# Gate projections of a decoder trunk as pairs of 64-row matmuls with two banks to add

## The chip, the cores and the metric

The kernel runs on one core of a Trainium2 chip. The metric is the device time of one execution in microseconds. The kernel before has a median of 1394.32 us over three runs (1393.59 to 1394.59).

## What is computed

Two decoder layers over 256 tokens of 1024 features, in float32. Each layer is a half-step feed-forward block, a mixing block and another half-step feed-forward block. The mixing block projects the normalised input with one matrix `w_in`, runs four causal mixers (`nsa`, `ret`, `rwkv`, `swa`) on column groups of the result, projects each mixer's output and sums the four under sigmoid gates. The gates are the last 4 x 1024 columns of the same projection:

```python
p = h @ w_in[l]
gates = sigmoid(c('branch_gate').reshape(B, S, N_BRANCH, D))
merged = (gates[:, :, 0] * (y_nsa @ w_br_nsa[l]) + gates[:, :, 1] * (y_ret @ w_br_ret[l])
          + gates[:, :, 2] * (y_rwkv @ w_br_rwkv[l]) + gates[:, :, 3] * (y_swa @ w_br_swa[l]))
x = x + rms_norm(merged @ w_out[l], mix_post_g[l])
```

## The kernel before

The tokens form two tiles of 128 (`t` = 0, 1). Normalised inputs are held transposed, features on partitions, as two tensors `xhi` and `xlo` of type F32R (lines 209 to 243): a float32 value is the sum of a high and a low part. Weights are streamed from memory in pieces of 128 x 1024 values (`stream`, line 131): a DMA on SyncE's queue into `raw`, then on ScalarE (ACT) a copy into the high part `whi` (line 146), then on VectorE (DVE) the difference `wlo` (line 147). A product of two such pairs is three matmuls that add into one PSUM bank, `mm3` (line 167): high x high (L173), high x low (L174) and low x high (L175).

`bulk_proj` (line 429) is the token-major projection. For each of the 8 chunks of 128 features and each token tile it calls `mm3` with the input as the stationary and 512 weight columns as the moving operand. The result of a token tile is one bank `pj`. When all chunks are in, `evac` takes it out of PSUM. `gate_block` (line 1306) is such a projection: its `evac` is one ACT operation, tanh of half the value, into the tile `gate` (L1309). Sigmoid(x) is 0.5 + 0.5 tanh(x / 2); `branch_block` (line 1313) multiplies its products `z` by gate + 1 on DVE (L1327, L1329) and `acc_split` brings in the factor 0.5 later. A gate block covers 512 columns of one mixer's gate, so there are 8 in each layer, 16 in all.

PSUM has eight banks, in two pools (lines 187 to 191): pool A with three, for projections and branch products, and pool B with five, for transposes, the strands' small products and the output rows (`dn`). A tile waits for a free bank of its pool.

The order of the mixing block is made in two steps. `weave` (line 453) emits work by an estimated clock, `clk`: strands of small, latency-bound products (attention, retention, the RWKV recurrence) as soon as their inputs should be there, and steps of bulk work in between. A projection gives back control after each chunk; `fin` notes when its result is expected. Gate blocks wait for nothing; a branch block waits for its mixer's output and its gate. The framework's scheduler then orders each engine's queue by priority, estimated times and free banks. Each engine runs its queue in that order.

The strands' products use operands of type F32 and often a part of the array: `rs`, `sc`, `lw` and `la` use 64 rows and 128 columns, `pz`, `pu`, `psn`, `py` and `pr` 64 rows and 64 columns. A matmul of F32 operands that is not a transpose shows as two records in the trace, one of F32R operands as one. The profile prints both types of stored operand as f32.

Of the kernel before, what the change touches and what calls it, by code (L numbers as in the profile page):

```python
# [12 lines left out]
AF = mybir.ActivationFunctionType  # L13
# [4 lines left out]
P = 128  # L18
# [9 lines left out]
RD = 1 / 32  # D ** -0.5  # L28
# [7 lines left out]
# per-feature vectors, features on partitions  # L36
V_MU, V_W0, V_A0, V_KK, V_KA, V_RK, V_POS = 0, 8, 10, 12, 14, 16, 18
NV = 18 + 32
# per-feature vectors, broadcast over partitions
# [73 lines left out]
class Trunk:  # L113
# [17 lines left out]
    def stream(self, src, k, n, part=None, between=None):  # L131
        """k chunks of 128 rows by n columns; returns w(chunk, columns) -> (hi, lo)"""
# [20 lines left out]
    def stream2(self, src, part):  # L153
        """one chunk of 1024 columns, its halves' parts in storage of 2 KiB each"""
# [12 lines left out]
    def mm3(self, out, a, b, first, last):  # L167
        """out (+)= a.T @ b with a, b given as (hi, lo) parts."""
        mm = self.nc.tensor.matmul
        d = 3 * max(109.0, 2.5 + b[0].shape[-1] / 2.4)  # L170
        self.clk += d
        self.light = max(0.0, self.light - d)
        mm(out, a[0], b[0], start=first, stop=False)  # L173
        mm(out, a[0], b[1], start=False, stop=False)  # L174
        mm(out, a[1], b[0], start=False, stop=last)  # L175

    def s2(self, shape, name, dt=F32):
        """a slot of up to 2 KiB per partition"""
# [4 lines left out]
    def k1(self, shape, name, dt=F32):  # L183
        """a slot of up to 1 KiB per partition"""
# [15 lines left out]
    def rstd(self, ss, k=1.0):  # L200
        """(sum(ss) + k * eps) ** -0.5 per token, of sums of k / D * x ** 2"""
# [14 lines left out]
    def pre_norm(self, t, xT, ss=None):  # L216
        """x[t] (token-major) -> normalised, transposed, as hi/lo [P, KC, token tile t]; returns the
        part from the transposes on, a step for each half."""
# [31 lines left out]
    def post_norm(self, t, banks, g, half, last):  # L250
        """x[t] += (0.5 if half else 1) * rms_norm(f) * g, f in two PSUM banks; sums of squares of the new x."""
# [28 lines left out]
    def ffn(self, l, wg, wu, wd, xT, post_g, nxt, mix=False, first=None):  # L280
        nc, tc = self.nc, self.tc
        with tc.tile_pool(name=self.nm("ffn"), bufs=1, reuse_waits="tile") as pool:
# [34 lines left out]
            # the first blocks are token-major, so that one token tile's products need not wait for the  # L317
            # other's input
# [53 lines left out]
    def rows_out(self, lhs, wd, g, half, nxt, units, tail, warm=None):  # L372
        """x += norm(lhs.T @ wd), rows of wd streamed in units of (chunks, storage of the parts); the last
        units one token tile after the other, so that the first tile's norms run under the second
        tile's products."""
# [39 lines left out]
    def warm(self, func):  # L415
        """have the table of the next phase's activations loaded while the engine has time"""
# [12 lines left out]
    def bulk_proj(self, l, xT, c0, n, evac, key, lat=900, skew=False):  # L429
        """token-major projection, activations stationary; one step per k-chunk."""  # L430
# [22 lines left out]
    def weave(self, strands, bulk):  # L453
        """Emit work in the order of an estimated clock: latency-bound strands as soon as their
        inputs should be there, bulk products in between."""
# [3 lines left out]
        while live or bulk or cur:  # L459
            ran = False  # L460
            # small products alone let the array's clock drop: bulk at least every so often
# [48 lines left out]
    def rope(self, out_ap, src, t, nh, dup=False):  # L510
        """src [P, nh, HD] (token-major) -> out_ap [P, nh, (2,) HD]."""
# [17 lines left out]
    def transposes(self, srcs):  # L529
        """up to four [P, P] blocks -> one PSUM bank [P, 4, P]."""  # L530
# [10 lines left out]
    def mm4(self, out, a, b):  # L541
        """few columns of b: the array's column groups side by side, as loading a holds them up"""
# [9 lines left out]
    def attention(self, t, groups, score, pv, sink, mask_off, gate, evac):  # L552
        """Groups of two softmaxes: score(g, scores in PSUM, W); pv(j, hh, pT): the pairs (V, p^T) whose
        products make up half hh of chunk j of o^T; evac(t, o^T in PSUM)."""
# [49 lines left out]
    def split_yt(self, yT, u, t, src, from_psum=True):  # L604
        """hi/lo parts of feature-major y (two chunks, one token tile)."""
# [9 lines left out]
    def swa(self, l, xT):  # L615
# [10 lines left out]
        def after(t):  # L626
            r = self.s2([P, 4, HD], "swar")
            # query heads land as 0, 2, 1, 3 so that a pair's halves meet kv heads 0 and 1
# [33 lines left out]
    def nsa(self, l, xT):  # L662
        """two projection blocks (bulk); spawns the strands that follow"""
# [5 lines left out]
        # queries: hi parts above lo parts; keys: hi and lo parts, each twice  # L669
# [81 lines left out]
        def cmp_prep():  # L751
            # 15 overlapping blocks plus position; the last chunk's columns run on into zeros
# [13 lines left out]
        def compress():  # L766
            yield "cmp_x"
            # column group 32 g holds chunks of parity g % 2 of the keys (g < 2) or the values
# [195 lines left out]
    def rwkv_proj(self, l, xT, b):  # L964
        """feature-major projection of 256 columns with token shift"""
# [22 lines left out]
    def rwkv(self, l):  # L988
# [8 lines left out]
        # decay, in-context rate and output gate from the low-rank inputs  # L997
# [20 lines left out]
        # cumulative log decay in each chunk, centred on the chunk's middle  # L1018
# [18 lines left out]
        # normalised removal keys, replacement keys  # L1037
# [44 lines left out]
        # strictly causal / causal interactions within each chunk: rows and columns of one chunk  # L1082
        # share a 64-partition half; units u = (token tile, head pair)
# [21 lines left out]
        # the inverted blocks, at most 32 wide, lie side by side: rows of group g, columns of its block  # L1105
# [27 lines left out]
        # token-major copies  # L1133
# [361 lines left out]
```

## Time and profile before

| what | value |
|---|---|
| median of three runs | 1394.32 us (1393.59 to 1394.59) |
| profiled execution, first to last instruction | 1397.0 us |
| its mean granted TensorE clock | 0.988 |
| PE busy (matmuls) | 1358.2 us, 97% |
| DVE busy | 846.6 us, 61% |
| ACT busy | 644.1 us, 46% |
| chain that ended last, PE's share | 79% |
| moved by DMA | 243.16 MB, mean 174 GB/s |

The profiled execution is known by its span alone; no other time of it is given. A busy share is an average over stages. The busy time of PE is made of modelled ends of overlapping matmuls, so the distance between the starts of two matmuls says more about PE than the duration of one. The mixing blocks run from about 200 to 490 us and from about 900 to 1180 us of the span; the gate tiles are written between 361.4 and 478.9 us and between 1052.8 and 1168.8 us.

### The profile page before, as it was taken

The numbers are of one execution on the slowest core, as the hardware profiler recorded it, in microseconds if no ns is written. First come the engines' busy times: TensorE is split into PE (matmuls) and PEld (weight loads), VectorE is DVE, ScalarE is ACT, GpSimd is POOL, SyncE is SP. The second block draws the span as 40 slices with busy tenths as digits, with TensorE's granted clock in tenths as the row PEclk, the third lists the DMA queues.
The fourth block names the chain that finished last, engine by engine and source line by source line (L and its number), as shares of the span: only waits on it lengthen the run. The fifth ranks groups of instructions, "written<-read, shape, count | busy, mean of one in ns | idle before, by whom it ended". The sixth has DMA issues, their size and how long they took to land.

```text
span 1397.0 us, 26502 instructions
## 1 busy us (share of the span) xinstructions
PE 1358.2 (97%) x10940; PEld 1205.1 (86%) x10940; DVE 846.6 (61%) x1269; ACT 644.1 (46%) x962; POOL 204.9 (15%) x269
## 2 busy tenths in 40 slices
PE   8999999899999999999999999999999999999998
PEld 8999879776778889998899998788777888899986
DVE  6555467758766666554565554677487656655543
ACT  5444456425344455444454444554353445544432
POOL 1000013513332110000000000235035320100000
PEclk9999999899999999999999999999999999999999
DMA  8866553436346546655657556443453565465552
GB/s 273 277 183 187 188 182 99 147 123 197 105 151 194 182 151 209 214 182 181 204 159 240 182 180 198 155 131 124 153 172 99 166 195 189 146 217 185 185 181 76
DMA packets 166153, 243.16 MB, mean 174 GB/s; under 512 B 9216, under 2 KB 120320, under 8 KB 165904
## 3 DMA queue, kind: packets, MB, share of 16 engines
q1 hardware_dynamic: 165248, 239.31, 53.9%
q8 instruction: 86, 1.41, 0.4%
q0 software_dynamic: 352, 1.10, 0.3%
q10 hardware_dynamic: 432, 1.05, 0.2%
q14 instruction: 35, 0.29, 0.1%
HBM read 240.38 MB, written 1.05 MB: 173 GB/s over the span
## 4 chain that ended last, share of the span: by engine, by line
PE 79%; DVE 9%; POOL 4%; ACT 3%; DMA 2%; issue 2%; POOLq 0%; DVEq 0%; SPq 0%; ACTq 0%
PE pg L175 7%; PE pg L173 7%; PE pg L174 7%; PE dn L173 6%; PE dn L175 6%; PE dn L174 6%; PE pj L173 5%; PE pu L174 5%; PE pu L173 5%; PE pu L175 5%; PE pj L175 5%; PE pj L174 5%; DVE wlo L147 2%; PE z L173 1%; PE tr L533 1%
## 5 line engine op out<-in xcount | busy, mean ns | idle before, releaser
L147 DVE TENSOR_TENSOR wlo<-raw,whi 128x1024 fp32r<-128x1024 f32 (+1 forms) x420 | 517.2, 1239 | 385.5 <-ACT whi L146 384.0
L146 ACT ACTIVATE whi<-raw 128x1024 fp32r<-128x1024 f32 (+1 forms) x420 | 436.3, 1046 | 543.7 <-issue 146.3
L173 PE MATMUL pj<-whi,xhi 128*128 128x512 f32 (+2 forms) x448 | 179.5, 401 | 0.4 <-DVE retg L894 0.4
L175 PE MATMUL pj<-whi,xlo 128*128 128x512 f32 (+2 forms) x448 | 173.1, 386 | 0.0
L174 PE MATMUL pj<-wlo,xhi 128*128 128x512 f32 (+2 forms) x448 | 172.6, 385 | 0.0
L173 PE MATMUL pu<-xhi,whi 128*128 128x256 f32 x592 | 168.1, 284 | 0.0
L173 PE MATMUL pg<-xhi,whi 128*128 128x256 f32 x592 | 168.1, 284 | 0.0
L174 PE MATMUL pu<-xlo,whi 128*128 128x256 f32 x592 | 167.8, 283 | 0.0
L175 PE MATMUL pg<-xhi,wlo 128*128 128x256 f32 x592 | 167.8, 283 | 0.0
L175 PE MATMUL pu<-xhi,wlo 128*128 128x256 f32 x592 | 167.8, 283 | 0.0
L174 PE MATMUL pg<-xlo,whi 128*128 128x256 f32 x592 | 167.8, 283 | 0.0
L174 PE MATMUL dn<-wlo,hhi 128*128 128x512 f32 x352 | 137.4, 390 | 0.0
L173 PE MATMUL dn<-whi,hhi 128*128 128x512 f32 x352 | 137.4, 390 | 0.0
L175 PE MATMUL dn<-whi,hlo 128*128 128x512 f32 x352 | 137.1, 390 | 0.0
L204 POOL TENSOR_SCALAR rstd<-ss 128x1 f32<-128x1 f32 x24 | 10.2, 427 | 807.5 <-ACT ja L258 780.3
L174 PEld LDWEIGHTS pg<-xlo,whi 128*128 128x128 f32 x592 | 113.8, 192 | 0.0
L174 PEld LDWEIGHTS pu<-xlo,whi 128*128 128x128 f32 x592 | 113.8, 192 | 0.0
L175 PEld LDWEIGHTS pg<-xhi,wlo 128*128 128x128 f32 x592 | 113.8, 192 | 0.0
L173 PEld LDWEIGHTS pg<-xhi,whi 128*128 128x128 f32 x592 | 113.8, 192 | 0.0
L173 PEld LDWEIGHTS pu<-xhi,whi 128*128 128x128 f32 x592 | 113.8, 192 | 0.0
L175 PEld LDWEIGHTS pu<-xhi,wlo 128*128 128x128 f32 x592 | 113.8, 192 | 0.0
L173 PEld LDWEIGHTS pj<-whi,xhi 128*128 128x128 f32 x448 | 86.2, 192 | 23.5 <-issue 6.6
(349 smaller groups left out, 2268.5 us busy)
## 6 DMA issues: line engine op xcount, KB each, us to landing
raw<-in_w_in_dram SPq DMA_DIRECT2D x112, 512.0 KB, 3.5
raw<-in_ffn_w_gate_dram SPq DMA_DIRECT2D x88, 512.0 KB, 4.5
raw<-in_ffn_w_up_dram SPq DMA_DIRECT2D x88, 512.0 KB, 4.3
raw<-in_ffn_w_down_dram SPq DMA_DIRECT2D x88, 512.0 KB, 3.7
raw<-in_w_out_dram SPq DMA_DIRECT2D x16, 512.0 KB, 3.6
cw<-in_nsa_cmp_k_w_dram SPq DMA_DIRECT2D x8, 512.0 KB, 3.9
cw<-in_nsa_cmp_v_w_dram SPq DMA_DIRECT2D x8, 512.0 KB, 4.5
raw<-in_w_br_ret_dram SPq DMA_DIRECT2D x8, 512.0 KB, 3.7
```

Source lines behind the costliest of these rows:

```text
L146: nc.scalar.activation(hi, raw, AF.Copy)
L147: nc.vector.tensor_sub(lo, raw, hi.bitcast(F32))
L173: mm(out, a[0], b[0], start=first, stop=False)
L174: mm(out, a[0], b[1], start=False, stop=False)
L175: mm(out, a[1], b[0], start=False, stop=last)
L204: eng.tensor_scalar(r, ss[:, 0:1], k * EPS, None, op0=ALU.add)
L533: self.nc.tensor.transpose(pt[:, j * P:(j + 1) * P], s, self.ident)
```

## The change

`gate_block` no longer calls `bulk_proj`. It streams the same weights and walks the chunks and token tiles in the same order, but each matmul over 128 rows becomes two over 64: partitions 0 to 63 (`e` = 0) and 64 to 127 (`e` = 1) of both operands. The two write whole banks of their own, one from pool A and one from pool B, each summed over all chunks. At the end ACT copies the first bank into the gate tile, DVE adds the second bank to it and ACT takes the tanh in place. The clock estimate for PE stays the same; the expected delay of the result goes from 900 to 1800. The rest of the difference removes comments and moves line numbers by 18.

```diff
     def gate_block(self, l, m, b, xT):
-        def evac(t, ps):
+        nc = self.nc
+        c0 = C_GATE + m * D + b * 512
+        w = [self.stream(self.A["w_in"][l][h * 512:(h + 1) * 512, c0:c0 + 512], 4, 512) for h in range(2)]
+        pp = [(self.psA("pj"), self.psB("pj")) for _ in range(NT)]
+        mm = nc.tensor.matmul
+        for c in range(KC):
+            wh, wl = w[c // 4](c % 4, slice(0, 512))
+            for t in range(NT):
+                ts_ = slice(t * P, (t + 1) * P)
+                for i, (x, v) in enumerate(((xT[0], wh), (xT[0], wl), (xT[1], wh))):
+                    for e in range(2):
+                        es = slice(64 * e, 64 * e + 64)
+                        mm(pp[t][e], x[es, c, ts_], v[es], start=c + i == 0, stop=c + i == KC + 1)
+                self.clk += 3 * (2.5 + 512 / 2.4)
+                self.light = max(0.0, self.light - 640)
+            yield
+        for t in range(NT):
             g = self.gt[m, b, t] = self.s2([P, 512], "gate")
-            self.nc.scalar.activation(g, ps, AF.Tanh, scale=0.5)
-        yield from self.bulk_proj(l, xT, C_GATE + m * D + b * 512, 512, evac, f"gate{m}{b}")
+            nc.scalar.activation(g, pp[t][0], AF.Copy)
+            nc.vector.tensor_add(g, g, pp[t][1])
+            nc.scalar.activation(g, g, AF.Tanh, scale=0.5)
+        self.fin(f"gate{m}{b}", 1800)
```

The order on PE where the first gate block of layer 1 begins; `pj_4143` and `pj_4144` are the two token tiles' banks before:

```order
L175 MATMUL pj_3795<-whi_3790,xlo_193 128x512
L173 MATMUL pj_4143<-whi_4121,xhi_192 128x512
L174 MATMUL pj_4143<-wlo_4122,xhi_192 128x512
L175 MATMUL pj_4143<-whi_4121,xlo_193 128x512
L538 MATMUL pu_4155<-mv_4093,TF_2893 64x64 x4
L533 MATMUL tr_4161<-ident,sm_3947 128x128 x4
```

The same place in the changed kernel; 4143 and 4144 are now the lower and upper half's banks of token tile 0, 4145 and 4146 those of token tile 1:

```order
L175 MATMUL pj_3795<-whi_3790,xlo_193 128x512
L1320 MATMUL pj_4143<-whi_4121,xhi_192 128x512
L1320 MATMUL pj_4144<-whi_4121,xhi_192 128x512
L1320 MATMUL pj_4143<-wlo_4122,xhi_192 128x512
L1320 MATMUL pj_4144<-wlo_4122,xhi_192 128x512
L1320 MATMUL pj_4143<-whi_4121,xlo_193 128x512
L1320 MATMUL pj_4144<-whi_4121,xlo_193 128x512
L1320 MATMUL pj_4146<-whi_4121,xhi_192 128x512
L1320 MATMUL pj_4146<-wlo_4122,xhi_192 128x512
L1320 MATMUL pj_4146<-whi_4121,xlo_193 128x512
L1320 MATMUL pj_4145<-whi_4121,xhi_192 128x512
L1320 MATMUL pj_4145<-wlo_4122,xhi_192 128x512
```

The halves alternate for token tile 0; for token tile 1 three products of the upper half stand ahead of three of the lower half.

The order on ACT at the last gate block of layer 1, before; `mh` are parts of the merged rows:

```order
L146 ACTIVATE whi_5443<-raw_5441 128x1024
L1309 ACTIVATE gate_5325<-pj_5275 128x512
L1309 ACTIVATE gate_5327<-pj_5276 128x512
L146 ACTIVATE whi_5449<-raw_5447 128x1024
L1399 ACTIVATE mh_5373<-tr_5375 128x512
```

And in the changed kernel:

```order
L146 ACTIVATE whi_5875<-raw_5873 128x1024
L1326 ACTIVATE gate_5753<-pj_5653 128x512
L1328 ACTIVATE gate_5753<-gate_5753 128x512
L1326 ACTIVATE gate_5757<-pj_5655 128x512
L146 ACTIVATE whi_5881<-raw_5879 128x1024
L1328 ACTIVATE gate_5757<-gate_5757 128x512
L1417 ACTIVATE mh_5805<-tr_5807 128x512
```

The copy out of the second token tile's bank stands behind the first tile's tanh, which reads what DVE adds.

The order on DVE at the same place, before; `gate_5247` and `gate_5249` belong to the gate block before the last, and `z` are the branch products:

```order
L147 TENSOR_TENSOR wlo_5444<-raw_5441,whi_5443 128x1024
L147 TENSOR_TENSOR wlo_5450<-raw_5447,whi_5449 128x1024
L1329 SCALAR_TENSOR_TENSOR gate_5247<-gate_5247,z_5335 128x512
L1329 SCALAR_TENSOR_TENSOR gate_5249<-gate_5249,z_5336 128x512
L1331 TENSOR_TENSOR acc_4605<-acc_4605,gate_5247 128x512
```

And in the changed kernel, where these two are `gate_5621` and `gate_5625`:

```order
L147 TENSOR_TENSOR wlo_5876<-raw_5873,whi_5875 128x1024
L1327 TENSOR_TENSOR gate_5753<-gate_5753,pj_5654 128x512
L1327 TENSOR_TENSOR gate_5757<-gate_5757,pj_5656 128x512
L147 TENSOR_TENSOR wlo_5882<-raw_5879,whi_5881 128x1024
L1347 SCALAR_TENSOR_TENSOR gate_5621<-gate_5621,z_5767 128x512
L1347 SCALAR_TENSOR_TENSOR gate_5625<-gate_5625,z_5768 128x512
L1349 TENSOR_TENSOR acc_4713<-acc_4713,gate_5621 128x512
```

The last gate's two additions now stand ahead of the operations that read the branch products of the gate before it.

## Rows read from the trace of the kernel before

**Rows 1.** The profile's page, its first line and part 1.
```profile
span 1397.0 us, 26502 instructions
...
PE 1358.2 (97%) x10940; PEld 1205.1 (86%) x10940; DVE 846.6 (61%) x1269; ACT 644.1 (46%) x962; POOL 204.9 (15%) x269
```

**Rows 2.** The page's part 4, the chain that ended last, by engine.
```profile
PE 79%; DVE 9%; POOL 4%; ACT 3%; DMA 2%; issue 2%; POOLq 0%; DVEq 0%; SPq 0%; ACTq 0%
```

**Rows 3.** Busy time by stretches; in brackets the number of instructions.
```profile
core 0: us, PE busy (x) PEld busy (x) DVE busy (x) ACT busy (x) POOL busy (x), PEclk, DMA share, GB/s
...
385.00:420.00 35.00, 33.47 (x197) 26.73 (x197) 22.64 (x45) 14.72 (x21) 10.50 (x9) 0.95 0.49 152
...
1085.00:1180.00 95.00, 94.75 (x467) 77.85 (x466) 58.28 (x74) 45.81 (x59) 20.19 (x14) 1.00 0.56 178
```

**Rows 4.** Groups by line and shape, PE; after the bar busy us, mean ns.
```profile
L173 PE MATMUL pj<-whi,xhi 128*128 128x512 f32 x384 | 156.3, 407 | 0.4 <-DVE retg L894 0.4
...
L538 PE MATMUL rg<-g,gs 128*128 128x256 f32 x8 | 2.1, 381 | 0.0
```

**Rows 5.** Timeline of PE inside a gate block; columns: start us, us.
```profile
1101.01 0.39 PE L174 MATMUL pj<-wlo,xhi 128*128 128x512 f32 x1
1101.23 0.39 PE L175 MATMUL pj<-whi,xlo 128*128 128x512 f32 x1
1101.46 0.39 PE L173 MATMUL pj<-whi,xhi 128*128 128x512 f32 x1
1101.69 0.39 PE L174 MATMUL pj<-wlo,xhi 128*128 128x512 f32 x1
```

**Rows 6.** Timeline of PE, 64-row products on both halves of the array.
```profile
228.69 0.38 PE L538 MATMUL lw<-tw,wa 64*128 64x256 f32 x1
228.70 0.47 PE L538 MATMUL la<-xl,wa 64*128 64x256 f32 x1
228.90 0.38 PE L538 MATMUL lw<-tw,wa 64*128 64x256 f32 x1
229.01 0.38 PE L538 MATMUL la<-xl,wa 64*128 64x256 f32 x1
229.12 0.38 PE L538 MATMUL lw<-tw,wa 64*128 64x256 f32 x1
```

**Rows 7.** Timeline of PE, whole-array products of F32 operands, four merged.
```profile
240.18 1.03 PE L538 MATMUL rg<-g,gs 128*128 128x256 f32 x4
```

**Rows 8.** Timeline of PE around products of other shapes in the first gate block.
```profile
356.70 0.39 PE L175 MATMUL pj<-whi,xlo 128*128 128x512 f32 x1
357.02 0.46 PE L538 MATMUL pz<-sst,ar 64*64 64x64 f32 x8
...
358.91 0.50 PE L173 MATMUL pj<-whi,xhi 128*128 128x512 f32 x1
359.24 0.40 PE L174 MATMUL pj<-wlo,xhi 128*128 128x512 f32 x1
```

**Rows 9.** Instructions on the tile gate; duration ns min/median/max, first and last start.
```profile
L1309 ACT ACTIVATE gate<-pj x32: 577/598/600, 361.4 to 1168.8; 128x512 f32<-128x512 f32 x32
L1329 DVE SCALAR_TENSOR_TENSOR gate<-gate,z x24: 673/680/682, 421.1 to 1174.5; 128x512 f32<-128x512 f32 x24
```

**Rows 10.** The page's part 5, the splits of the weights.
```profile
L147 DVE TENSOR_TENSOR wlo<-raw,whi 128x1024 fp32r<-128x1024 f32 (+1 forms) x420 | 517.2, 1239 | 385.5 <-ACT whi L146 384.0
L146 ACT ACTIVATE whi<-raw 128x1024 fp32r<-128x1024 f32 (+1 forms) x420 | 436.3, 1046 | 543.7 <-issue 146.3
```

**Rows 11.** Timeline of PE, the last strand's transposes and those of the merged rows.
```profile
1105.55 0.38 PE L533 MATMUL tr<-ident,yrwkv 128*128 128x128 f32 x2
...
1174.21 1.04 PE L533 MATMUL tr<-ident,acc 128*128 128x128 f32 x8
```

**Rows 12.** Timeline of PE's weight loads (PEld) in the gate block of rows 5.
```profile
1101.01 0.19 PEld L175 LDWEIGHTS pj<-whi,xlo 128*128 128x128 f32 x1
1101.24 0.19 PEld L173 LDWEIGHTS pj<-whi,xhi 128*128 128x128 f32 x1
```

## The prediction

> **What bounds the kernel now.** The page's first part comes first: TensorE's matmuls are busy 97% of a span of 1397.0 us, VectorE 61%, ScalarE 46% [rows 1]. Then the chain that ended last: 79% of it is PE, 9% DVE, 3% ACT [rows 2]. So a change pays or costs by what it does to the matmul stream. The table by stretches says the same of the stage that is changed: in the two stretches where most gate blocks lie, the matmuls are busy 33.47 of 35 us and 94.75 of 95, while DVE has 12 and 37 us free and ACT 20 and 49 [rows 3]. Extra work on DVE and ACT has room there; extra time on PE has none.
>
> The mean duration of a product with 512 columns is 407 ns [rows 4], but products overlap. Their price is the distance between starts: four in a row start at 1101.01, .23, .46 and .69, so 0.68 us for three, **0.227 us each** [rows 5]. The 16 gate blocks (4 mixers, 2 halves, 2 layers) have 48 such products each: 768, some 174 us in all.
>
> The profiled span is 2.7 us (0.2%) above the median of the runs, 1394.32 us. I work out a difference and add it to the median; on the span's own scale everything is 2.7 us higher. A difference under 0.2%, 2.8 us, can't be told from none here.
>
> **The change, part by part.**
>
> *The products.* Each of the 768 becomes two of 64 rows, 1536 in all, all with 512 columns. If both halves of the array work at once, a pair should take about one old turn; if not, two. The kernel already has 64-row products in the same 64x128 form, with operands stored as plain F32: `lw` on one half of the rows and `la` on the other. `lw` starts at 228.69, 228.90 and 229.12, one every 0.215 us, and `la` runs beside it from 228.70 and again from 229.01 [rows 6]. So the halves do work at once. Whole-array products of the same stored type and 256 columns, `rg`, also take (1.03 - 0.38) / 3 = 0.217 us each, 0.38 being the length of one [rows 4, 7]. Pairing therefore neither adds to nor takes from the turn; the stored type sets it. The gate operands are F32R, and an F32R turn is 0.227. I take **0.227 per pair, a difference of 0**. Bounds: 0.216, the turn of the F32 pairs, gives 768 x -0.011 = -8.4 us; 0.227 plus the 0.01 by which the second half starts later [rows 6] gives +7.7 us. The value taken is the row with the same type, number of columns and rate.
>
> *Switching between array shapes.* A product of 64x128 next to one of another shape has a price. `pj` at 356.70 is followed by a 64x64 product at 357.02, 0.32 us instead of 0.23: 0.09 more. Where the whole array is used again, at 358.91, the next product starts only at 359.24, 0.33 instead of 0.23: 0.10 more, since the first weights after a switch were not loaded ahead [rows 8]. Together 0.19 us a switch. Counted over the built program's matmuls, neighbours with different shapes go from 170 to 208: the gates used to have the shape of the other projections, the branch products and the transposes, and no longer do. 38 x 0.19 = **+7.2 us**, all on PE. Bounds: 38 x 0.09 = 3.4, if the other half hides the first load, and 7.6.
>
> *Pairs that are pulled apart.* The scheduler separates 20 of the 1536 from their partners. At each layer's first gate block, three lower-half products stand in a row and then three upper-half ones (the first of the orders shown above): five turns instead of three, as the first upper one can run beside the last lower one. Four more pairs are split by another product, one turn each. 2 x 2 + 4 = 8 turns x 0.227 = **+1.8 us**.
>
> *Evacuation.* A gate tile was one ACT operation of 598 ns [rows 9]. Now it is an ACT copy, a DVE add and an ACT tanh. DVE's row with one operand in PSUM and 512 columns is 680 ns [rows 9]. So ACT gains 32 x 0.598 = 19.1 us, DVE 32 x 0.680 = 21.8 us. Their cover is the free time above [rows 3]; were it gone, these would be the price. What is not covered is order. On ACT the second tile's copy stands behind the first tile's tanh, which waits for DVE (the second order). Its bank of pool A comes free 0.598 + 0.680 + 0.598 + 0.598 = 2.5 us after the first tile's products, against 1.2 before. A weight split that gets in between adds 1.24 us on DVE or 1.05 on ACT [rows 10]: 4.8 us at worst, 4.1 after the second tile's products. The next branch block takes pool A's third bank and the first tile's, the one after it needs this bank: 12 products, 2.7 us, later. That is a wait of 0 to 1.4 us at six places (three mixers with 12-product blocks, two layers), 0 to 8.2 us. On DVE the adds also stand ahead of the operations that free the branch banks (the third order), so I don't take 0, but 0.5 us a place: **+3.0 us**. The gates also hold two of the five banks of pool B; that delays strands, whose last result (the RWKV transposes of layer 2 at 1105.55) stands 70 us before the mixing block's end [rows 11], so 0.
>
> *Loads* are the same on every queue, and POOL's work doesn't change.
>
> **Sum:** 0 + 7.2 + 1.8 + 3.0 = 12.0 us. 1394.3 + 12.0 = **1406.3 us**, 0.9% slower (1409.0 on the span's scale).
>
> **The rivals.**
>
> *Pairs remove the start-up of a product.* The 11 ns that F32R's turn has above F32's could be a start-up that one half spends while the other streams. Then the products give -8.4 us, the first load after a switch is hidden the same way (3.4), the split pairs stay (1.8), and with half my evacuation term the sum is -8.4 + 3.4 + 1.8 + 1.5 = -1.7: 1392.6 us, 1391 to 1397 by what the evacuation and the switches take. With side costs of 6.7 it decides below 0.227 - 6.7 / 768 = 0.218 us a pair. For it: no row has F32R on half the array, and the plain type's turn is 0.216. Against it: 64 and 128 rows of the plain type have the same turn [rows 6, 7], which shows no start-up that halves would hide. The Trainium skill (TensorE: Matmul & The Clock Gate, Part 3) says that a weight load overlaps running matmuls only where their row groups differ; by that rule halves would hide loads that whole-array products show, and this rival's time would hold. The trace disagrees as far as it goes: whole-array loads start as the product before theirs does, at 1101.01 and 1101.24, and last 0.19 us, inside the turn of 0.227 [rows 12].
>
> *The halves get in each other's way.* If each pair pays F32R's start-up once more, its turn is 0.237 or a little more: 7.7 + 12.0 = +19.7, 1414.0 us; with the upper bounds of all terms 7.7 + 7.6 + 1.8 + 8.2 = +25.3, 1419.6 us.
>
> *F32R doesn't run on both halves at once.* Then the change doesn't do what it says: each pair takes two turns, 768 x 0.227 = +174.3, with the 12.0 some 1581 us. Two full-rate streams into two banks are shown by no row: the F32 products need 0.216 us for 256 columns, so they write half as fast. Against it are their starts 0.01 us apart [rows 6].
>
> **How the numbers follow.** My forecast (pair at 0.224 to 0.232): 0.43, 1402 to 1410 us, a tenth of it lower where the waits vanish. Start-up removed: 0.23, half of that past the 0.2% line at 1391.5, the rest within it or just above. In each other's way: 0.14. One half at a time: 0.14. Something else, slower: 0.06. So faster 0.12, same (1391.5 to 1397.1) 0.18, slower 0.70. The range 1391 to 1420 leaves out the serial case and a little below, under 2 in 10; it reaches from the low bound 1394.3 - 8.4 + 3.4 + 1.8 = 1391.1 to the high one.
>
> **What would show it.** The gate products of a pair starting some 0.01 us apart and the next pair 0.227 after: right; 0.216, 0.237 or 0.45 name the rival. Switches: about 0.1 us more before and after each change of shape. Waits of PE for ACT copies or DVE operations on branch tiles: some 3 us. I would be wrong if the pair's turn falls to 0.216 or doubles, or if the page shows PE idle by over 8 us more at the branch blocks.

## The result, and the profile after

The changed kernel takes 1418.74 us (median; 1417.48 to 1421.14) beside 1394.45 us of the kernel before on the same chip: ratio 1.0165, 95% interval 1.0147 to 1.0182, **24 us slower**. Forecast were 12 us more, 1406.3, range 1391 to 1420: the side and the range hold, the size is half of what was measured. The profiled executions differ by less, 1415.7 against 1397.0 us, 18.7. Every other run here has a span some 1.8 us under its time, so the profiled execution of the kernel before took an estimated 1398.8 us, 4.4 above its median. One execution of experiment 2, 1420.92 us at a granted clock of 0.973, fell in a slower state and is left out of its ratio.

The page after, its first line, part 1 and the chain that ended last, by engine:

```profile
span 1415.7 us, 28126 instructions
...
PE 1370.9 (97%) x11708; PEld 1211.0 (86%) x11708; DVE 867.6 (61%) x1301; ACT 661.9 (47%) x994; POOL 200.9 (14%) x269
...
PE 79%; DVE 10%; ACT 4%; POOL 3%; issue 2%; DMA 1%; POOLq 0%; DVEq 0%; SPq 0%; ACTq 0%
```

The page hardly moves against [rows 1, 2]: PE is still at 97%, with 768 more matmuls and only 12.7 us more of busy time. Where the time went shows only in the stage itself. The table by stretches, from the first gate product to the first product of `w_out`, for both layers, of the kernel before:

```profile
341.94:485.69 143.75, 140.77 (x856) 114.06 (x854) 94.46 (x183) 61.29 (x84) 38.37 (x28) 0.99 0.52 161
1032.94:1175.54 142.60, 140.08 (x856) 113.76 (x854) 93.55 (x177) 60.90 (x83) 38.37 (x28) 0.99 0.51 163
sum 286.35, PE 280.85 PEld 227.82 DVE 188.01 ACT 122.19 POOL 76.74; mean PE 140.42 PEld 113.91 DVE 94.01 ACT 61.09 POOL 38.37
```

and of the changed one (columns as in [rows 3]: length, then PE, PEld, DVE, ACT and POOL busy, PEclk):

```profile
339.33:494.42 155.09, 148.04 (x1240) 116.91 (x1239) 106.33 (x201) 69.72 (x100) 36.49 (x28) 0.98 0.47 150
1040.99:1194.92 153.93, 147.92 (x1240) 119.04 (x1239) 104.91 (x196) 69.56 (x100) 36.50 (x28) 0.98 0.47 151
sum 309.02, PE 295.96 PEld 235.95 DVE 211.24 ACT 139.28 POOL 72.99; mean PE 147.98 PEld 117.97 DVE 105.62 ACT 69.64 POOL 36.49
```

The stage is 309.02 - 286.35 = 22.7 us longer, 11.3 a layer, and the rest of the execution 4.0 us shorter: the change's cost is in this stage, but not all of the 22.7 is cost. PE's idle time in the stage rises from 5.5 to 13.1 us, by 7.6. The list of PE's waits in layer 1's gate stage names them, before:

```profile
PE z L173 <- DVE acc L1327: 1.5, 1, 1.5
PE pr L538 <- DVE yret L928: 0.8, 1, 0.8
PE pj L173 <- DVE retg L894: 0.4, 1, 0.4
```

just ahead of that stage, also before:

```profile
PE tr L533 <- DVE sm L584: 2.7, 1, 2.7
```

and in the stage after:

```profile
PE pj L1320 <- DVE retg L894: 2.3, 1, 2.3
PE tr L533 <- DVE cp L849: 1.4, 1, 1.4
PE z L173 <- DVE gate L1347: 0.7, 2, 0.6
PE tr L533 <- DVE yl L609: 0.7, 1, 0.7
PE z L173 <- DVE acc L1345: 0.7, 1, 0.7
PE pu L538 <- DVE rz L1228: 0.4, 1, 0.4
...
PE pz L538 <- DVE yrwkv L1284: 0.3, 1, 0.3
PE py L538 <- DVE yret L928: 0.2, 1, 0.2
```

Almost every wait is for DVE. The longest, for `retg`, is the first gate block's own: it waits for a bank of pool A that `retg` still holds. In layer 1 it takes the place of the wait for `sm`, of which 0.4 us are left after, so some 2.3 of the 22.7 us only moved into the stage; in layer 2 `sm` keeps its 2.7 us and the wait for `retg` is 1.1, where there was none. Most of the other new ones are products of strands (`tr`, `pu`, `pz`: compressed attention, RWKV), not gate or branch products: 3.0 us in layer 1 and 3.1 in layer 2, against 0.8 in each before. That is the first sign that the missing half isn't where I had put it.

The products themselves did what was forecast. The timeline of PE in a gate block of layer 2 shows merged pairs, one every 0.22 to 0.24 us. Over all gate products of the trace the median distance from one pair to the next is 0.227 us, the same as for the whole products before:

```profile
1109.86 0.49 PE L1320 MATMUL pj<-whi,xhi 64*128 64x512 f32 x2
1110.20 0.39 PE L1320 MATMUL pj<-wlo,xhi 64*128 64x512 f32 x2
1110.43 0.40 PE L1320 MATMUL pj<-whi,xlo 64*128 64x512 f32 x2
1110.66 0.40 PE L1320 MATMUL pj<-whi,xhi 64*128 64x512 f32 x2
```

Here 0.34 us lie between the first pair, after a switch of shape, and the next.

### The profile page after: what moved, and what is told of

It reads as the page before. It is cut to its first block, busy times and chain, and to the rows that moved or that the text cites. A ratio compares the mean times of both kernels' runs of the same rounds, so it can differ in the third digit from the quotient of the medians.

```text
span 1415.7 us, 28126 instructions
## 1 busy us (share of the span) xinstructions
PE 1370.9 (97%) x11708; PEld 1211.0 (86%) x11708; DVE 867.6 (61%) x1301; ACT 661.9 (47%) x994; POOL 200.9 (14%) x269
## 4 chain that ended last, share of the span: by engine, by line
PE 79%; DVE 10%; ACT 4%; POOL 3%; issue 2%; DMA 1%; POOLq 0%; DVEq 0%; SPq 0%; ACTq 0%
PE pj L1320 11%; PE pg L173 7%; PE pg L175 7%; PE pg L174 7%; PE dn L173 6%; PE dn L174 6%; PE dn L175 6%; PE pu L173 5%; PE pu L174 5%; PE pu L175 5%; DVE wlo L147 2%; PE pj L173 2%; PE pj L175 2%; PE pj L174 1%; PE tr L533 1%
## 5 line engine op out<-in xcount | busy, mean ns | idle before, releaser
L1320 PE MATMUL pj<-whi,xhi 64*128 64x512 f32 x512 | 119.0, 401 | 3.4 <-DVE retg L894 3.4
L1320 PE MATMUL pj<-wlo,xhi 64*128 64x512 f32 x512 | 116.3, 389 | 0.0
L1320 PE MATMUL pj<-whi,xlo 64*128 64x512 f32 x512 | 115.8, 389 | 0.0
L175 PEld LDWEIGHTS dn<-whi,hlo 128*128 128x128 f32 x352 | 66.1, 188 | 13.7
```

Of the source, the lines that this page charges most:

```text
L1320: mm(pp[t][e], x[es, c, ts_], v[es], start=c + i == 0, stop=c + i == KC + 1)
```

## The experiments

"Theory" in a text below means the one held when that run was made; it changed twice. Ratios are to the kernel before on the same chip in the same session; in us they are taken of 1394.4.

### 1. Evacuation and banks, with whole-array products

Forecast: 3.0 us for the waits that the copy, the add and the second bank bring. The first run keeps both and goes back to whole-array products.

```diff
-                    for e in range(2):
-                        es = slice(64 * e, 64 * e + 64)
-                        mm(pp[t][e], x[es, c, ts_], v[es], start=c + i == 0, stop=c + i == KC + 1)
+                    mm(pp[t][c // 4], x[:, c, ts_], v, start=c % 4 + i == 0, stop=c % 4 + i == 5)
```

> Whole-array products as before, but chunks 0 to 3 sum into the first bank and 4 to 7 into the second, with the evacuation of the changed kernel. No 64-row product and no change of array shape is added (174 neighbours of different shapes, 170 before), so this shows evacuation and banks alone. Theory (switches, evacuation and waits share the cost, a pair costs one old turn): 1398 to 1402 us. Rival 1 (evacuation and the held banks are most of the 24 us): 1409 or more. Rival 2 (64-row products are slower than the starts show, 0.03 us a pair): 1394 to 1397.

Measured: 1397.16 us, ratio 1.000 (0.9985 to 1.0016). But here the first bank is complete half a block early, which can hide its copy. A later run closes that gap with even chunks in one bank and odd ones in the other:

```diff
-                    mm(pp[t][c // 4], x[:, c, ts_], v, start=c % 4 + i == 0, stop=c % 4 + i == 5)
+                    mm(pp[t][c % 2], x[:, c, ts_], v, start=c // 2 + i == 0, stop=c // 2 + i == 5)
```

> Whole-array gate products again (768, shapes as before, about 170 switches), but even chunks of rows sum into the first bank and odd chunks into the second, so that both banks are complete only with the block's last products, as in the change. The evacuation is the change's: copy, add, tanh. In the run with chunks 0 to 3 in the first bank that bank was complete half a block early, which may have hidden its copy; here nothing hides it. TensorE's order comes out close to the one of the kernel before (the transposes of cp behind 17 turns of gate products). Theory E, late banks and evacuation cost the missing time: 1408 to 1415 us, ratio 1.010 to 1.014. Theory O, the order that the scheduler gives to 1536 products costs it: 1394 to 1400, ratio 1.000 to 1.003.

Measured: 1393.93 us, ratio 0.9989 (0.998 to 0.9999). With whole-array products the evacuation and the four banks cost nothing; Theory E, as a cost by itself, falls.

### 2. The price of a switch

One half of the array alone, no second bank, the old evacuation. The upper 64 rows' part of each gate is left out:

```diff
-        pp = [(self.psA("pj"), self.psB("pj")) for _ in range(NT)]
+        pp = [self.psA("pj") for _ in range(NT)]
...
-                    for e in range(2):
-                        es = slice(64 * e, 64 * e + 64)
-                        mm(pp[t][e], x[es, c, ts_], v[es], start=c + i == 0, stop=c + i == KC + 1)
+                    mm(pp[t], x[0:64, c, ts_], v[0:64], start=c + i == 0, stop=c + i == KC + 1)
...
-            nc.scalar.activation(g, pp[t][0], AF.Copy)
-            nc.vector.tensor_add(g, g, pp[t][1])
-            nc.scalar.activation(g, g, AF.Tanh, scale=0.5)
+            nc.scalar.activation(g, pp[t], AF.Tanh, scale=0.5)
-        self.fin(f"gate{m}{b}", 1800)
+        self.fin(f"gate{m}{b}", 900)
```

> Leaves out the upper 64 rows of each gate product: 768 products of 64 rows into one bank, evacuated by one tanh as before. It has 202 neighbours of different array shapes, 32 more than before. Theory: 32 x 0.19 = 6.1 us above before, 1399 to 1402 us, though half the multiplications are gone. Rival 1 (evacuation and banks): 1394 to 1396. Rival 2 (each 64-row product costs extra): some 12 us above before, 1406.

Measured: 1402.02 us, ratio 1.0028 (1.001 to 1.0045): 3.9 us for 32 more switches, 0.12 each (0.04 to 0.20), if nothing else differs. The other side: even chunks of rows as pairs, odd ones whole, with 72 more switches than the change.

```diff
+                    if c % 2:
+                        mm(pp[t][0], x[:, c, ts_], v, start=False, stop=c + i == KC + 1)
+                        continue
                     for e in range(2):
                         es = slice(64 * e, 64 * e + 64)
-                        mm(pp[t][e], x[es, c, ts_], v[es], start=c + i == 0, stop=c + i == KC + 1)
+                        mm(pp[t][e], x[es, c, ts_], v[es], start=c + i == 0, stop=e == 1 and c + i == KC)
```

> Even chunks as pairs of halves, odd chunks as whole-array products into the first bank; same evacuation. 280 neighbours of different shapes, 72 more than in the changed kernel, and half as many pairs. Theory: 72 x 0.19 = 13.7 us above the changed kernel, 1429 to 1433 us. If only the 0.09 us ahead of a switch counts: 1425. Rival 2 (cost goes with the number of pairs): 12 us below it, 1407.

Measured: 1435.49 us, ratio 1.0277 (1.0254 to 1.0299), 15.6 us above the change: 0.22 a switch (0.16 to 0.27 by the two intervals), again if nothing else differs. Its timeline shows the two halves of the price, 0.33 us into the pairs and 0.34 behind the first pair, where a turn is 0.23:

```profile
1150.69 0.40 PE L1319 MATMUL pj<-whi,xlo 128*128 128x512 f32 x1
1151.02 0.50 PE L1323 MATMUL pj<-whi,xhi 64*128 64x512 f32 x2
1151.36 0.39 PE L1323 MATMUL pj<-wlo,xhi 64*128 64x512 f32 x2
1151.59 0.40 PE L1323 MATMUL pj<-whi,xlo 64*128 64x512 f32 x2
```

So the row-based price of 0.19 stands between the two, and 38 switches are 4.6 to 8.2 us.

### 3. Halves pulled apart

Three products of the lower half in a row, then three of the upper, everywhere; PE's queue in the built program has them so in all but a few places:

```diff
-                for i, (x, v) in enumerate(((xT[0], wh), (xT[0], wl), (xT[1], wh))):
-                    for e in range(2):
-                        es = slice(64 * e, 64 * e + 64)
+                for e in range(2):
+                    es = slice(64 * e, 64 * e + 64)
+                    for i, (x, v) in enumerate(((xT[0], wh), (xT[0], wl), (xT[1], wh))):
                         mm(pp[t][e], x[es, c, ts_], v[es], start=c + i == 0, stop=c + i == KC + 1)
```

> Same products and banks, but for each chunk and token tile the three of the lower half stand first and then the three of the upper half. Theory (the queue runs in order, so the halves work together only where neighbours are of different halves): four turns for each three pairs, 256 x 0.227 = 58 us above the changed kernel, 1473 to 1479 us. Rival (products of the idle half run ahead of those that wait for the other): 1417 to 1421 us.

Measured: 1421.95 us, ratio 1.017 (1.0147 to 1.0192), the change's own time. My theory asked for 58 us more and is wrong. PE's timeline shows the same pairs as if they had been written as pairs; a row merges two products whose starts lie 10 ns apart:

```profile
1119.88 0.40 PE L1320 MATMUL pj<-whi,xlo 64*128 64x512 f32 x2
1120.11 0.40 PE L1320 MATMUL pj<-whi,xhi 64*128 64x512 f32 x2
1120.34 0.40 PE L1320 MATMUL pj<-wlo,xhi 64*128 64x512 f32 x2
```

### 4. TensorE's order

The scheduler places the strands' products among the gate products, and the change shows it twice as many of those. In the kernel before, nine gate products stand between the four `ro` products and the two transposes of `cp`, nine turns; in the changed kernel three half-array products, two turns. My theory was that this order makes the waits. Both kernels with PE in the order in which the program writes:

```diff
-            self.weave([self.rwkv(l)], bulk)
+            with tc.manual_schedule(engines={mybir.EngineType.PE}):
+                self.weave([self.rwkv(l)], bulk)
```

> The changed kernel with TensorE's instructions in the order in which the program writes them down, instead of the order that the scheduler picks; the sums, banks and evacuation are those of the change. Neighbours of different array shape: 194. My theory: of the 24 us that the change costs, the part that is not switches comes from strand products (transposes of cp and yrwkv, pu, pz, py, ro) that the scheduler puts too early in TensorE's order because it counts the 1536 half products as twice the time. Against the kernel before with the same order (the other run of this call) only the switches are left: 194 - 166 = 28 times 0.17 to 0.19 us = 5 us, a ratio between the two of 1.003 to 1.006. Rival: the pairs and their banks cause the waits whatever the order; then the two differ by 15 us or more, ratio 1.011 and up. Against the kernel before with its own order I expect no fixed value: the written order may itself cost or save.

> The kernel before with TensorE's instructions in the order in which the program writes them down; nothing else is changed. 166 neighbours of different array shape, 4 fewer than in the scheduler's order. It is the base for the run of the changed kernel with the same order: my theory gives 5 us between the two, the rival 15 or more. By itself it shows what the scheduler's order is worth without the change: if the written order lets products wait for their strands, it is slower than the kernel before by those waits; I expect between no change and 15 us slower.

Measured: 1423.55 us with the change, ratio 1.0189 (1.0172 to 1.0206), and 1405.09 us without, 1.0056 (1.0042 to 1.007). 18.5 us lie between them, not 5, so the theory as stated falls: more than switches is left. But the two written orders aren't the same, and the run can't rule PE's order out: from the `cpo` products on, the strands' products stand in other places among the gate and branch products. Announcing a finished gate 900 ns later isn't the reason, since the run of experiment 5 announces it as before and has the change's places. The change also lowers the program's second count, `light`, from which `weave` decides when strands may run, by 640 for three products where `mm3` lowers it by 647.5; built with 647.5, the strands there stand nearly as they do in the kernel before. By itself this costs nothing: the two runs of experiment 1 have it, at ratios of 1.000 and 0.9989.

The run without the change shows what PE's order does with no pair in it. Its written order puts the transposes of `cp` right behind the four `ro` products, and the second token tile's first gate products right behind the first tile's, as the change does. PE's waits in layer 1 of that run:

```profile
PE pj L173 <- DVE retg L894: 2.1, 1, 2.1
PE tr L533 <- DVE cp L849: 1.5, 1, 1.5
```

These are the change's two longest waits, 2.3 and 1.4 us, with whole-array products; layer 2 has 0.5 and 1.5, where the change has 1.1 and 1.4. So PE's order is enough to bring these two.

### 5. Pairs with the old evacuation

```diff
-            nc.scalar.activation(g, pp[t][0], AF.Copy)
-            nc.vector.tensor_add(g, g, pp[t][1])
-            nc.scalar.activation(g, g, AF.Tanh, scale=0.5)
-        self.fin(f"gate{m}{b}", 1800)
+            nc.scalar.activation(g, pp[t][0], AF.Tanh, scale=0.5)
+        self.fin(f"gate{m}{b}", 900)
```

> The changed kernel with its 1536 half-array products into two banks, in the scheduler's order of the change, but with the evacuation of the kernel before: one tanh of the first bank on ACT, no copy and no add; the second bank, with the sums of the upper 64 rows, is not read. This leaves out the upper rows' part of each gate. Theory E, late banks and evacuation cost the missing time: only the switches are left, 1398 to 1404 us, ratio 1.003 to 1.007, as in the run with the lower half alone. Theory O, the order: 1412 to 1420, ratio 1.013 to 1.018, with the waits for cp, yrwkv and rz where the changed kernel has them. If both matter, each run gives a part and the two parts add up to the 17 to 20 us that are not switches.

Measured: 1411.45 us, ratio 1.0115 (1.0101 to 1.0129): between the two theories. In the change the evacuation is worth (1.0165 - 1.0115) x 1394.4 = 7.0 us (some 4 to 10 by the intervals), 8 switches of it, some 1.5, included; with whole-array products it was worth nothing (1). And the upper half's products, which give no operation on ACT or DVE more than the run with the lower half alone, cost (1.0115 - 1.0028) x 1394.4 = 12.1 us although they run beside the lower half's. The banks that they hold cost nothing with whole-array products (1). PE's waits in layer 1 of the lower half alone:

```profile
PE pu L538 <- DVE rz L1228: 1.2, 1, 1.2
PE pj L1318 <- DVE retg L894: 0.8, 1, 0.8
```

and of this run, with both halves:

```profile
PE pj L1320 <- DVE retg L894: 2.3, 1, 2.3
PE py L538 <- DVE yret L928: 1.9, 1, 1.9
PE tr L533 <- DVE cp L849: 0.9, 1, 0.9
PE tr L533 <- DVE yl L609: 0.7, 1, 0.7
```

The strand waits are there without the change's evacuation. What differs between the two programs, besides the products in the other half, is what the scheduler did on all three engines. On PE, nine gate products stand between `ro` and the transposes of `cp` in the run of the lower half alone, as in the kernel before, and none in this run. DVE's order differs too, with the same operations in it (a weight split `wlo` moves ahead of the maximum `cmx` from which `cp` follows, the four `yret` operations ahead of the first sum of `yacc`).

### 6. Strands later, and the copies first

If waits for strands are a matter of order, strands that are written later among the gate products must lose them:

```diff
-                        s[0] = self.clk + r
+                        s[0] = self.clk + r + self.slack
...
     def gate_block(self, l, m, b, xT):
...
+        self.slack = 1500.0
...
```

> The changed kernel in which a strand that resumes during the gate blocks is written down 1.5 us later on the program's own clock. In TensorE's order the strands' products then stand behind more gate products (the transposes of cp behind 12 turns of gate products after csc and ro no longer close by), and 222 neighbours have different array shapes, 14 more than in the change (+2 to 3 us). Products, banks and evacuation are the change's. Theory O: the change's waits for strand results (cp, yret, yrwkv, rz, yl; about 2 us of idle time a layer that the profile shows and some 2.5 more that it hides behind the end of the product before) are a matter of the order, so they go: 1408 to 1414 us, ratio 1.009 to 1.014. Rival: pairs make TensorE wait wherever the strands stand; then no gain, and the added switches give 1419 to 1423, ratio 1.017 to 1.020.

> The kernel before with the same edit: strands that resume during the gate blocks are written down 1.5 us later. 188 neighbours of different shape, 18 more than before (+2 to 3.5 us), and fewer waits for yret and acc (up to 2 us a layer to be had). Expected 1392 to 1398, ratio 0.998 to 1.003; if it is below 0.998, the edit itself is an improvement that needs no pairs. The difference between the two runs of this call should be 34 switches of 0.12 to 0.19 us and what is left of the evacuation, 7 to 14 us, where the order of the scheduler gives 24.

Measured: 1434.78 us with the change, ratio 1.0276 (1.0252 to 1.0299), and 1403.4 us without, 1.0058 (1.0039 to 1.0077). The total with the change is a miss for both theories, and the run without it, expected at 1392 to 1398 us, misses too. The list of waits of layer 1 says why. The waits for `yret`, `yrwkv`, `rz` and `yl` are gone and that for `cp` with them, and a larger one has come:

```profile
PE z L173 <- ACT gate L1327: 5.6, 1, 5.6
PE psn L538 <- DVE sd L909: 1.1, 1, 1.1
PE z L173 <- DVE gate L1348: 0.9, 2, 0.6
```

The timelines of ACT and DVE of the same run show its chain; in brackets the idle time before a row and who ended it:

```profile
386.37 0.60 ACT L1327 ACTIVATE gate<-pj 128x512 f32<-128x512 f32 x1 [3.13 <-PE pj L1321]
393.80 0.63 ACT L1329 ACTIVATE gate<-gate 128x512 f32<-128x512 f32 x1 [6.84 <-DVE gate L1328]
395.29 0.58 ACT L1327 ACTIVATE gate<-pj 128x512 f32<-128x512 f32 x1
...
391.81 1.37 DVE L928 TENSOR_SCALAR yret<-ro,bmv,rs 128x128 f32<-128x128 f32 x4 [1.79 <-POOL rs L197]
393.09 0.68 DVE L1328 TENSOR_TENSOR gate<-gate,pj 128x512 f32<-128x512 f32 x1
```

The rise isn't all waiting: the granted clock is 0.978 to 0.983 in this run's executions and 0.987 to 0.989 in the change's, on average 0.007 lower, which over 1435 us is some 10 us of full speed. The gate's add (L1328) stands behind the retention strand's `yret` on DVE, which waits for POOL. ACT's tanh (L1329) waits 6.84 us for the add, the second tile's copy (L1327) stands behind that tanh, and the branch block waits on PE for the bank that this copy frees. Two more runs take that chain apart. First the change with both copies ahead of the tanh operations:

```diff
-        for t in range(NT):
-            g = self.gt[m, b, t] = self.s2([P, 512], "gate")
-            nc.scalar.activation(g, pp[t][0], AF.Copy)
-            nc.vector.tensor_add(g, g, pp[t][1])
-            nc.scalar.activation(g, g, AF.Tanh, scale=0.5)
+        with self.tc.manual_schedule(engines={mybir.EngineType.Activation}):
+            for t in range(NT):
+                g = self.gt[m, b, t] = self.s2([P, 512], "gate")
+                nc.scalar.activation(g, pp[t][0], AF.Copy)
+            for t in range(NT):
+                g = self.gt[m, b, t]
+                nc.vector.tensor_add(g, g, pp[t][1])
+                nc.scalar.activation(g, g, AF.Tanh, scale=0.5)
```

> The changed kernel with ACT's order in the evacuation pinned: both tiles' copies first, then the two tanh operations, so that the second tile's bank of pool A no longer waits for the first tile's add on DVE. Everything else is the change's (204 neighbours of different shape). The evacuation costs some 7 us here by the run with the old evacuation. If that is the chain on ACT (copy behind tanh behind add), the time falls to 1411 to 1414 us, ratio 1.011 to 1.013. If it is DVE's 32 adds standing ahead of the strands' operations (cp, yret, yrwkv), nothing changes: 1416 to 1420, ratio 1.015 to 1.018, and the waits for strand results stay.

Measured: 1416.56 us, ratio 1.0138 (1.0121 to 1.0155), 3.8 us less than the change's ratio gives, with intervals that overlap a little: between the two expectations, so that neither chain is shown to be the whole 7 us. The strand waits stay (1.7 us for `yret`, 0.9 for `cp`, 0.7 for `yl`). Then later strands with the old evacuation, which has no such chain on ACT:

> Pairs with the strands 1.5 us later and with the evacuation of before (one tanh of the first bank; the sums of the upper 64 rows are left out). 218 neighbours of different shape. With the strands later and the change's evacuation the strand waits were gone, but one wait of 5.6 us a layer came for a bank of pool A. Theory: strand waits are a matter of the order, and that wait is the evacuation's; here both are gone and only switches stand against the kernel before with the same edit (1.0058): 30 times 0.12 to 0.20 us = 4 to 6 us, 1406 to 1411 us, ratio 1.008 to 1.011. Rival: pairs make TensorE wait in either order; then 16 us stay, as with the old evacuation in the scheduler's order: 1417 or more, ratio 1.016 and up.

Measured: 1426.11 us, ratio 1.0203 (1.0188 to 1.0218). The time is the rival's; the mechanism is neither's. The strand waits of the change are gone, and one wait of 4.3 us in each layer, for DVE, is in their place. DVE's timeline ahead of it:

```profile
391.13 1.36 DVE L928 TENSOR_SCALAR yret<-ro,bmv,rs 128x128 f32<-128x128 f32 x4 [1.80 <-POOL rs L197]
392.41 0.47 DVE L1228 TENSOR_TENSOR rz<-pz,mv 64x128 f32<-64x128 f32 x2
392.81 1.21 DVE L147 TENSOR_TENSOR wlo<-raw,whi 128x1024 fp32r<-128x1024 f32 x1
393.94 1.27 DVE L1344 SCALAR_TENSOR_TENSOR acc<-gate,z 128x512 f32<-128x512 f32 x2
```

The branch block's evacuation (L1344), which frees the `z` banks, stands behind strand operations and a weight split. It is one queue: when strands come early, PE waits for their results; when they come late, gates and branches wait behind them on DVE.

## Why the prediction was right and where it fell short

**The products, 0: right.** A pair takes the old turn, 0.227 us; the rivals with 0.216, 0.237 or two turns are all out. The time came close to the 1414 us of the rival in which the halves get in each other's way, but by another mechanism. That 1418.7 lies within the range is luck in part: my own mechanism was put at 1402 to 1410, and the range's top, 1420, was made of that rival's 7.7 us, which didn't come, and of the upper bounds of the other terms.

**The switches, +7.2: right in size.** 0.12 to 0.22 us each, where 0.19 was taken from [rows 8]. In the gate stage there are 18 more a layer (44 where there were 26), 36 x 0.20 = 7.2 of its 22.7 us; the 0.20 is what the timeline of experiment 2 shows.

**Pairs pulled apart, +1.8: about right in size, one of its two reasons wrong.** Experiment 3 pulls all of them apart and costs nothing measurable, so three products of one half ahead of three of the other don't take five turns. But where a bank is late or another product stands between, halves do run alone. In the first gate block the upper half's three products of the second token tile run, then PE waits for the lower half's bank:

```profile
340.59 0.39 PE L1320 MATMUL pj<-whi,xlo 64*128 64x512 f32 x1
343.25 0.49 PE L1320 MATMUL pj<-whi,xhi 64*128 64x512 f32 x1 [2.26 <-DVE retg L894]
```

That is six turns for three pairs, in each layer, and two more pairs a layer are split by `cp` and by a branch block: 10 turns of 0.227 us beyond those of the pairs, 2.3 us.

**Evacuation and bank waits, +3.0 of 0 to 8.2, and "that delays strands, ... so 0": the step that failed.** The mechanism named, a copy behind a tanh that waits for DVE and a branch block that waits for the bank, exists (experiment 6), but in the change it is a small part. Taken out of the change, the evacuation is worth 7.0 us, 1.5 of them switches (experiment 5), within the 0 to 8.2, but not by that wait: of the 6.7 us of waits listed in layer 1, `z` has 1.4, no more than the 1.5 it had before. What I had set to 0 is the greater part: strands with 70 us of slack at their end [rows 11] were taken as harmless, yet their products stand in PE's own order, and a product whose strand is late holds up every gate product behind it. The kernel before had a sign of it, 0.8 us of waiting for `yret` in each layer, in stretches that [rows 3] leaves out (of layer 1's 144 us it shows 35). Idle time in the stage rises by 7.6 us, 4.5 of it in waits for strands and 3.0 in the wait for `retg`'s bank. With the old evacuation there are still 16 us to pay (experiment 5), of which 30 more switches are 4 to 7.

**A term that was missing: the clock.** The gate stage before already lost some at half clock (1.2 GHz in place of 2.4): a granted clock of 0.95 over 35 us in the first stretch of [rows 3]. After the change it loses more, in both layers in the stretch with the long waits:

```profile
340.00:375.00 35.00, 31.36 (x301) 25.36 (x298) 24.41 (x70) 13.38 (x24) 1.74 (x2) 0.91 0.34 106
1041.00:1076.00 35.00, 32.50 (x305) 26.20 (x305) 23.81 (x67) 13.87 (x25) 2.24 (x2) 0.90 0.33 106
```

(0.09 + 0.10) x 35 = 6.7 us of full speed lost, against 0.05 x 35 in each layer before (in layer 2 over 1028 to 1063 us), 3.5: some 3 us more. Two single executions can't size it, but the runs agree: the median granted clock is 0.991 in the executions of the kernel before, and the change's four have 0.987 to 0.989, which is 3 to 6 us. In layer 1 a part of it lies behind a wait. The timeline of PE after the transposes of `cp`, which waited 1.37 us:

```profile
370.60 0.41 PE L533 MATMUL tr<-ident,cp 128*128 128x128 f32 x2 [1.37 <-DVE cp L849]
...
372.29 3.68 PE L538 MATMUL ro<-retv,sd 128*128 128x128 f32 x16
```

The granted clock from 372.5 to 375.7 us is 0.50. The same 16 products in the run of experiment 5, which had no drop there:

```profile
372.90 2.05 PE L538 MATMUL ro<-retv,sd 128*128 128x128 f32 x16
```

**The sum of the gate stage:** 7.2 for switches, 7.6 of idle time, 3.1 of clock: 17.9 of 22.7, and with the 2.3 of halves that ran alone 20.2. Of the remaining 2.5 a part is what a wait costs beyond its shown idle time: at `cp` the gate product before starts at 368.83 and a turn of 0.23 would end at 369.06, but the idle time counts from the modelled end 0.39 after the start, 0.16 us later. With six more waits in layer 1's list, and as many in layer 2, that is an estimated 1.9 us. The rest, 0.6, is less than these terms are known to. The 2.3 us that moved into the stage are in its idle time.

**What is shown, and what stays open.** PE's order is enough for the waits for `cp` and for `retg`'s bank: the kernel before has both when its products stand in that order (experiment 4). That the scheduler gives such an order to 1536 products and not to 768 of them is what experiments 2 and 5 show, `cp` behind nine gate products or behind none. The evacuation alone isn't it (experiments 1 and 5). What makes the other strands late (`yl`, `yret`, `yrwkv`, `rz`) stays open. The runs fit an order on DVE and ACT that the scheduler built with gate products counted twice, but a run with all three engines' orders held equal in both kernels wasn't made.

## What to carry to other kernels

Splitting a 128-row product into two 64-row products on both halves of the array buys no time where a whole product already keeps the same turn; here it paid twice, in switches of shape of about 0.2 us each and in what the larger number of instructions and a longer evacuation did to the order of in-order queues, which these runs show in part. When a change alters the number of instructions on the engine that bounds, go through the waits of the strands that share its queue, also of those with slack at their end. To test an evacuation, keep the rest of the old program with it: by itself it was free here, in the changed program it was worth some 7 us. And before two programs in written order are compared, see that the written orders are the same.

## What the runs showed of the hardware that I had not expected

Products of the idle half run ahead of earlier ones that wait for the other half: with three of one half and three of the other in PE's queue the pairs still start 10 ns apart, one each 0.23 us (experiment 3), and the time is that of written pairs (1421.95 against 1418.74 us). The Trainium skill (TensorE: Matmul & The Clock Gate, Part 3, The mechanism) says that matmuls start strictly in program order; by that rule three and three would need four turns for every three pairs, an estimated 58 us more. The measurement differs and decides here.
